# Second attention layer: exponentials transposed by DMA instead of by TensorE, its other DMAs issued by GpSimd

## The chip, the cores and the metric

The kernel runs on one core of one Trainium2 chip. The metric is the device time of one execution in microseconds (us). Engines: TensorE (PE, matmuls; its weight loads are PEld), VectorE (DVE), ScalarE (ACT), GpSimd (POOL) and SyncE (SP), which issues DMAs. All share 16 DMA engines.

## The reference

A model of 1024 tokens with width 1024: one layer with two kinds of attention (differential, and sparse with the 256 best keys), one layer with latent attention (MLA), a norm, and a block of its own with Fourier mixing, windowed attention and 16 experts. The change lies in the second of these, the MLA layer:

```
def block(args):                       # 128 queries; 16 heads
    s = (jnp.einsum('bqhd,bkhd->bhqk', qn, k_nope)
         + jnp.einsum('bqhr,bkr->bhqk', qr, k_rope)).astype(jnp.float32) * scale
    s = jnp.where(chunk_mask(qpos, kpos), s, -jnp.inf)
    p = jax.nn.softmax(s, axis=-1)
    return jnp.einsum('bhqk,bkhd->bqhd', p.astype(v.dtype), v)
...
return x + (o * jax.nn.silu(gate)) @ w_o
```

All in 32 bits. The kernel keeps that accuracy by splitting numbers into a high and a low half: matmuls with fp32r halves take three products, and the product of the exponentials with V has both as pairs of fp16.

## The kernel before

Function `layer1` projects the layer's inputs and stores queries, keys, values and gates in HBM. Then it runs over 16 heads. For each head it loads queries and keys into buffers that alternate between even and odd heads (`load_stack`, L852, and L1212 to L1220), and every fourth head the values (L1223). A head has 8 blocks of 128 queries; block qb sees qb + 1 blocks of keys, so 36 blocks of 128x128 in all. They are taken in five packs (`PACK1`: 7; 6 and 0; 5 and 1; 4 and 2; 3), of 8, 8, 8, 8 and 4 blocks. For each pack:

- TensorE multiplies queries and keys (L293, three products, PSUM banks of 128x512);
- VectorE adds the mask, finds the row maximum and writes the scores to the tile `e` in SBUF (L317; three buffers of `e`);
- ScalarE takes the exponential in place, with the row sum (L1247);
- `p_to_T` transposes `e`: TensorE turns up to four blocks into a PSUM tile `ptp` (L340, 32-bit), ScalarE casts it to fp16 as the high half `pTh` (L341), VectorE subtracts that and writes the rest as the low half `pTl` (L342);
- `pv_mm` multiplies with V: high by high, high by low, low by high (L350 to L352).

Other work is put between the packs: matmuls of the gates (`gate_units`), the preparation of the output weights (`prep_wo`), half of the output product (`half_units`, with loads by `gated_lhs`), bias rows for the next block (`bias_rows`), and modulation rows (`total` in `ada_rows`: load `adx`, one matmul, store to `mod_d`, over one buffer). Every load and store of this stretch is issued by SyncE, in the order of its queue; an instruction that waits holds up those behind it. The order on all engines is made by the framework's scheduler from the order in the text. GpSimd has no work in the heads.

The changed stretch runs from the first loads of keys to the last modulation row, about 1060 to 1490 us of the span.

Of the kernel before, what the change touches and what calls it, by code (L numbers as in the profile page):

```python
# [11 lines left out]
F32 = mybir.dt.float32  # L12
# [82 lines left out]
class K:  # L95


    def __init__(self, ctx, tc):
        self.tc = tc
        self.nc = tc.nc  # L100
        self.ctx = ctx
        self.n = 0
        self.const = ctx.enter_context(tc.tile_pool(name="const", bufs=1))
        self.small = ctx.enter_context(tc.tile_pool(name="small", bufs=3))
        self.dram = ctx.enter_context(tc.tile_pool(name="dscr", bufs=1, space=DRAM))
        nc = self.nc
        self.ident = self.const.tile([P, P], F32, name="ident")
        make_identity(nc, self.ident)
        self.ones = self.const.tile([P, P], F32, name="ones")
        nc.vector.memset(self.ones, 1.0)  # L110
        self.zeros = self.const.tile([P, 1], BF16, name="zeros")
        nc.vector.memset(self.zeros, 0.0)
# [96 lines left out]
    def load_w(self, pool, src, c_list, nk=NK, tag="w", scale=None, hl=None, raw_bufs=1, bufs=None, parts=1):  # L209

        nc = self.nc
        n = sum(w for _, w in c_list)
        if hl is None:
            hl = HL(pool, [P, nk, n], self.nm(tag), tag=tag, bufs=bufs)
        m = nk // parts
        for k0 in range(0, nk, m):
            raw = pool.tile([P, m, n], F32, tag=tag + "_raw", name=self.nm(tag + "raw"), bufs=raw_bufs)
            o = 0
            for c, w in c_list:
                nc.sync.dma_start(raw[:, :, o:o + w], src[k0 * P:(k0 + m) * P, c:c + w].rearrange("(k p) n -> p k n", p=P))  # L220
                o += w
            if scale is None:
                self.split(hl[:, k0:k0 + m], raw)
                continue
            for k in range(m):
                h, l, s = hl.hi[:, k0 + k, :], hl.lo[:, k0 + k, :], scale[:, k0 + k:k0 + k + 1]
                nc.scalar.activation(h, raw[:, k, :], AF.Copy, scale=s)
                nc.vector.scalar_tensor_tensor(l, raw[:, k, :], s, h.bitcast(F32), op0=ALU.mult, op1=ALU.subtract)
        return hl
# [114 lines left out]


def pv_mm(kk, out, hi, lo, v1, v2, nb, off=0):

    mm = kk.nc.tensor.matmul
    for j in range(nb):
        mm(out, hi[:, j, :], v1(off + j), start=j == 0, stop=False)  # L350
        mm(out, hi[:, j, :], v2(off + j), start=False, stop=False)  # L351
        mm(out, lo[:, j, :], v1(off + j), start=False, stop=j == nb - 1)  # L352
# [89 lines left out]
def bias_rows(kk, ps, rel_bias, onehot, heads, ncol, kdim, tag, mul, last=None):  # L442
# [8 lines left out]
    def unit(h, pool):  # L451
        if h == 0:
            rb = at["rb"] = pool.tile([P, heads], F32, name=tag + "rb")
            nc.sync.dma_start(rb[0:32, :], rel_bias)
            nc.vector.tensor_scalar(rb[0:32, :], rb[0:32, :], mul, None, op0=ALU.mult)
            if last is not None:
                nc.vector.memset(rb[32:33, :], last)
            oh = at["oh"] = pool.tile([P, 512], F32, name=tag + "oh")
            nc.sync.dma_start(oh[0:kdim, 0:L + 1], onehot)
        rb, oh = at["rb"], at["oh"]  # L460
# [5 lines left out]
        nc.scalar.copy(sb[:, :L], pb[:, :L])  # L466
        nc.sync.dma_start(scr[h], sb[:, :L])

# [288 lines left out]
def gate_units(kk, ps, pool, W, c0, hT, gate_d, first=None):  # L757
# [15 lines left out]
    def split(c, half):  # L773
        pp, sl = project(first[0] + P * c, half)
        hl = [pool.tile([P, 512], F32, tag="gth", name=kk.nm("gth"), bufs=2).bitcast(F32R) for _ in range(2)]
        kk.split(HL.of(*hl), pp)
        for z, d in zip(hl, first[1]):
            nc.sync.dma_start(d[P * c:P * c + P, sl], z.bitcast(F32))

    def unit(c, half):  # L780
# [3 lines left out]
        nc.vector.scalar_tensor_tensor(th, th, 1.0, pp, op0=ALU.add, op1=ALU.mult)  # L784
        nc.sync.dma_start(gate_d[P * c:P * c + P, sl], th)

# [61 lines left out]
def load_stack(kk, pool, src, row0, tag, lo_first=False, into=None, cols=slice(0, S)):  # L848

    t = pool.tile([P, cols.stop - cols.start], F32R, tag=tag, name=kk.nm(tag), bufs=2) if into is None else into  # L850
    for z in range(2):
        kk.nc.sync.dma_start(t[64 * z:64 * z + 64, :].bitcast(F32), src[z ^ int(lo_first)][row0:row0 + 64, cols])  # L852
    return t
# [17 lines left out]
def load_bias(kk, pool, bias_d, h, ncol, into=None):  # L871
    t = pool.tile([P, ncol], F32, tag="bias", name=kk.nm("bias")) if into is None else into
    L = bias_d.shape[2]
    v = bias_d[h].rearrange("p l -> (p l)")[P - 1:P - 1 + P * (L - 1)].rearrange("(p l) -> p l", l=L - 1)[:, :ncol]
    kk.nc.sync.dma_start(t, v)
    return t
# [28 lines left out]
def prep_wo(kk, pool, w, W, ks, scale=None, colB=None, bufs=2):  # L905
# [6 lines left out]
    def unit(i):  # L912
        for j in range(len(raws), min(i + bufs, len(ks))):
            raws[j] = pool.tile([P, D], F32, tag="woraw", name=kk.nm("woraw"), bufs=bufs)
            nc.sync.dma_start(raws[j], W[ks[j] * P:(ks[j] + 1) * P, :])
        raw, k = raws[i], ks[i]
# [12 lines left out]
def half_units(kk, ps, op, w, lhs, resid, dst):  # L929
# [5 lines left out]
    def unit(t, n):  # L935
# [7 lines left out]
        x = op.tile([P, 512], F32, tag="hx", name=kk.nm("hx"), bufs=2)  # L943
        nc.sync.dma_start(x, resid[rows, cols])
        po = ps.tile([P, 512], F32, tag=MM_BANK[0], name=kk.nm("poh"), bufs=MM_BANK[1])
        for k in range(4):
            kk.mm3(po, lt[t](k), w[k][:, cols], k == 0, k == 3)
        nc.vector.tensor_tensor(x, po, x, op=ALU.add)
        nc.sync.dma_start(dst[rows, cols], x)

# [42 lines left out]
def gated_lhs(kk, ps, op, mix_d, gate_d, k0, bank):  # L993
# [3 lines left out]
    def lhs(t):  # L997
        rows = slice(t * P, (t + 1) * P)
        mx = op.tile([P, 4, P], F32, tag="mx", name=kk.nm("mxt"), bufs=2)
        mv = mix_d[rows, k0 * P:k0 * P + 512].rearrange("p (k c) -> p k c", c=P)  # L1000
        nc.sync.dma_start(mx[:, 0:3], mv[:, 0:3])
        nc.sync.dma_start(mx[:, 3:4], mv[:, 3:4])
        g = op.tile([P, 4, P], F32, tag="gt", name=kk.nm("gtt"), bufs=2)
        nc.sync.dma_start(g, gate_d[k0 * P:k0 * P + 512, rows].rearrange("(k p) s -> p k s", p=P))

# [28 lines left out]
def layer1(kk, ps, a, hT, hold, mix_d, gate_d, wo, mod, wx):  # L1034
# [152 lines left out]
    px.close()  # L1187

    mod2, rows = mod
    ax = ExitStack()  # L1190
# [3 lines left out]
    for i in range(2):  # L1194
        for z in range(2):
            nc.sync.dma_start(kp[64 + 32 * z:96 + 32 * z, i, :].bitcast(F32), kr_d[0])
    k3 = kp[:, 2, :]
    nc.gpsimd.memset(k3[0:64].bitcast(F32), 0.0)
    for z in range(2):
        nc.sync.dma_start(k3[64 + 32 * z:96 + 32 * z, :].bitcast(F32), kr_d[1])  # L1200

# [5 lines left out]
    for h in range(16):  # L1207
# [3 lines left out]
        for z in range(2):  # L1211
            nc.sync.dma_start(k1[64 * z:64 * z + 64, :].bitcast(F32), kn_d[0][r0:r0 + 64, :])  # L1212
        q2 = ap_.tile([P, S], F32R, tag="q2", name=kk.nm("q2"))
        nc.sync.dma_start(q2[0:64, :].bitcast(F32), qn_d[0][r0:r0 + 64, :])
        for i in range(2):
            for z in range(2):
                b = 64 + 32 * i + 16 * z
                nc.sync.dma_start(q2[b:b + 16, :].bitcast(F32), qr_d[z][i][16 * h:16 * h + 16, :])
        k2 = kp[:, h % 2, :]
        at_ = nc.sync.dma_start(k2[0:64, :].bitcast(F32), kn_d[1][r0:r0 + 64, :]).ins  # L1220
        if h % 4 == 0:
            with kk.tc.issue_after(lk[-1]) if h else ExitStack():
                nc.sync.dma_start(vh[:, :, :, r0:r0 + 256], v_d[:, :, :, r0:r0 + 256])  # L1223
        lk.append(at_)
# [4 lines left out]
        for i, pack in enumerate(PACK1):  # L1229
            parts = offsets(pack)  # L1230
            n = parts[-1][2]
            e = ap_.tile([P, S], F32, tag="p", name=kk.nm("e"), bufs=3)
            mx = kk.sm([P, 2], tag="mxc")
# [12 lines left out]
            for z, (qb, c0, c1) in enumerate(parts):  # L1246
                nc.scalar.activation(e[:, c0:c1], e[:, c0:c1], AF.Exp, bias=nm[:, z:z + 1], scale=CS, accum_out=st[:, qb:qb + 1])  # L1247
            hi, lo = p_to_T(kk, ps, ap_, e, n // P)
            for qb, c0, c1 in parts:
# [14 lines left out]
        if h % 2:  # L1264
            nc.sync.dma_start(mix_d[:, (h // 2) * P:(h // 2 + 1) * P].rearrange("(t p) c -> p t c", p=P), o)
        if h == GATES1_HEADS - 1:
# [5 lines left out]
    halves.run()  # L1272
    mod2.run(None, mp)
    ax.close()
    hx.close()

def ada_rows(kk, ps, a, mod_d):
# [4 lines left out]
    c = kk.sm([P, NK], tag="ada_c", bufs=1)  # L1282
    nc.sync.dma_start(c, a["c_2"].rearrange("o (k p) -> p (o k)", p=P))
    th = kk.sm([P, NK], tag="ada_t", bufs=1)
# [7 lines left out]
    def unit(o, ap_, bufs):  # L1292
        acc = ap_.tile([P, H], F32, tag="acc", name=kk.nm("acc"))
        for q in range(0, NK, 2):
            w = ap_.tile([P, 2, H], F32, tag="adw", name=kk.nm("adw"), bufs=bufs)
            nc.sync.dma_start(w, a["w_ada_2"][q * P:(q + 2) * P, o:o + H].rearrange("(k p) n -> p k n", p=P))
            for k in range(2):
# [8 lines left out]
    def total(s, z, dst, gname, ap_):  # L1306
        o = s * D + z * H
        x = ap_.tile([P, H], F32, tag="adx", name=kk.nm("adx"))
        nc.sync.dma_start(x, part_d[:, o:o + H])
        b = ap_.tile([1, H], F32, tag="mb", name=kk.nm("mb"))  # L1310
        nc.sync.dma_start(b, a["b_ada_2"][:, o:o + H])
        pm = ps.tile([P, 512], F32, tag=MM_BANK[0], name=kk.nm("pm"), bufs=MM_BANK[1])
# [4 lines left out]
        if gname:  # L1317
            nc.sync.dma_start(b, a[gname][:, z * H:z * H + H])
            nc.vector.scalar_tensor_tensor(x[0:1, :], x[0:1, :], 1.0, b, op0=ALU.add, op1=ALU.mult)
        nc.sync.dma_start(mod_d[dst:dst + 1, z * H:z * H + H], x[0:1, :])  # L1320

# [847 lines left out]
```

## Time and profile before

| | us |
|---|---|
| median of 3 runs | 2592.82 (2587.34 to 2599.93) |
| the profiled execution | 2589.32 |
| its span, first to last instruction | 2587.5 |
| TensorE busy | 2355.9 (91%) |
| VectorE busy | 1797.5 (69%) |
| ScalarE busy | 1347.5 (52%) |
| GpSimd busy | 438.7 (17%) |
| mean granted TensorE clock | 0.950 |

Busy time is the union of an engine's instructions; issuing DMAs and waiting for semaphores don't count as busy. The clock is given as a share of full speed. A DMA share is the mean busy share of the 16 DMA engines.

### The profile page before, as it was taken

How to read it: one execution, taken by the hardware profiler on the slowest of the kernel's cores; microseconds unless marked ns; L12 is line 12 of the kernel's file. 1: busy time of each engine (PE TensorE's matmuls, PEld its weight loads, DVE VectorE, ACT ScalarE, POOL GpSimd, SP SyncE). 2: the span in 40 equal slices, each digit the busy share in tenths (PEclk: the TensorE clock that was granted, in tenths of full speed). 3: DMA queues.
4: the chain of work that ended last, by engine and by line, in shares of the span. 5: the costliest groups of instructions: out<-in, count | busy, mean ns of one | idle time of the engine just before them, and what ended most of it. 6: DMA issues, size and time to landing. Idle time of an engine off the chain costs nothing.

```text
span 2587.5 us, 40940 instructions
## 1 busy us (share of the span) xinstructions
PE 2355.9 (91%) x14412; PEld 1843.1 (71%) x14412; DVE 1797.5 (69%) x4575; ACT 1347.5 (52%) x2635; POOL 438.7 (17%) x626
## 2 busy tenths in 40 slices
PE   7988888898998878999989979989985999999998
PEld 6866666676777866788767768877864777777776
DVE  4459987877986355366776674677666777777775
ACT  4345675455653333255564375355452666666664
POOL 0000147757740013100000000011000101110110
PEclk9999888899999899999999989989997999999999
DMA  4442476566656227854776461545684999999994
GB/s 131 127 135 79 135 204 184 158 188 191 188 154 208 78 99 258 260 147 123 182 192 170 133 204 55 137 111 163 190 302 184 347 382 351 358 363 374 359 353 137
DMA packets 302637, 523.80 MB, mean 202 GB/s; under 512 B 46022, under 2 KB 191582, under 8 KB 302432
## 3 DMA queue, kind: packets, MB, share of 16 engines
q1 hardware_dynamic: 287456, 467.70, 55.5%
q0 software_dynamic: 14976, 53.49, 6.6%
q8 instruction: 114, 1.87, 0.3%
q14 instruction: 91, 0.75, 0.1%
HBM read 405.18 MB, written 115.65 MB: 201 GB/s over the span
## 4 chain that ended last, share of the span: by engine, by line
PE 61%; DMA 15%; DVE 10%; issue 4%; POOL 4%; ACT 4%; SPq 1%; POOLq 0%; DVEq 0%; ACTq 0%
PE sb L139 6%; PE sb L140 6%; PE sb L141 6%; PE sb L293 5%; PE ptp L340 3%; DMA adw<-w_ada 3%; PE w_gate L1815 2%; PE w_down L1815 2%; PE w_up L1815 2%; DVE tkj L397 2%; PE w_gate L139 2%; PE w_gate L141 2%; PE w_up L139 2%; PE w_up L141 2%; PE w_up L140 2%
## 5 line engine op out<-in xcount | busy, mean ns | idle before, releaser
L341 ACT CAST pTh<-ptp 128x512 f16<-128x512 f32 (+2 forms) x316 | 166.1, 557 | 134.8 <-PE ptp L340 129.0
L342 DVE TENSOR_TENSOR pTl<-ptp,pTh 128x512 f16<-128x512 f32 (+2 forms) x316 | 199.9, 648 | 38.1 <-ACT pTh L341 37.4
L1683 DVE TENSOR_TENSOR ring_l<-mraw,ring_h 128x1024 fp32r<-128x1024 f32 x152 | 183.8, 1223 | 33.6 <-ACT ring_h L1682 31.0
L340 PE MATMUL ptp<-ident,e 128*128 128x128 f32 x1184 | 182.2, 284 | 7.6 <-DVE e L670 2.1
L1682 ACT CAST ring_h<-mraw 128x1024 fp32r<-128x1024 f32 x152 | 156.4, 1048 | 59.0 <-PE w_up L141 20.8
L1683 DVE TENSOR_TENSOR ring_l<-xraw,ring_h 128x1024 fp32r<-128x1024 f32 x136 | 164.7, 1223 | 29.4 <-ACT ring_h L1682 27.0
L1682 ACT CAST ring_h<-xraw 128x1024 fp32r<-128x1024 f32 x136 | 140.7, 1049 | 46.2 <-PE w_up L141 19.9
L340 PEld LDWEIGHTS ptp<-ident,e 128*128 128x128 f32 x1184 | 133.4, 144 | 20.2 <-issue 4.0
L1247 ACT ACTIVATE e<-e,nmx 128x1024 f32<-128x1024 f32 (+7 forms) x128 | 98.4, 770 | 74.5 <-DVE nmx L1245 74.3
L352 PEld LDWEIGHTS <-pTl 128*128 128x128 f16 x1184 | 108.5, 99 | 35.6 <-issue 15.0
L350 PEld LDWEIGHTS <-pTh 128*128 128x128 f16 x1184 | 110.2, 100 | 30.9 <-issue 21.4
L1772 POOL DMA_INDIRECT xg<-h_d,idx x16 | 24.0, 1502 | 598.5 <-DVE gate L1775 550.7
L1298 POOL TENSOR_SCALAR adw<-adw,ada_s 128x256 f32<-128x256 f32 x192 | 109.1, 580 | 93.1 <-DMA adw<-w_ada 92.4
L902 ACT ACTIVATE e<-e,nmx 128x1024 f32<-128x1024 f32 (+7 forms) x128 | 98.5, 772 | 42.7 <-DVE nmx L901 23.4
L351 PEld LDWEIGHTS <-pTh 128*128 128x128 f16 x1184 | 110.0, 99 | 3.9 <-issue 3.2
L293 PE MATMUL sb<-hold_l,q 128*128 128x512 f32 (+3 forms) x384 | 104.0, 359 | 2.0 <-DMA q<-qr 2.0
L317 DVE CUSTOM_DVE_ANT_0 e<-sb,hide 128x512 f32<-128x512 f32 (+3 forms) x128 | 74.5, 583 | 37.6 <-PE sb L293 20.8
L139 PE MATMUL pg<-hold_h,wg_h 128*128 128x512 f32 x192 | 85.7, 446 | 16.3 <-DVE gth L135 14.1
L139 PE MATMUL w_down<-ring_h,hTm_h 128*128 128x512 f32 x192 | 91.3, 476 | 0.0
L139 PE MATMUL w_up<-ring_h,xT_h 128*128 128x512 f32 x192 | 90.3, 470 | 0.0
L139 PE MATMUL w_gate<-ring_h,xT_h 128*128 128x512 f32 x192 | 89.1, 464 | 0.0
L1950 POOL DMA_DIRECT2D xb_d<-x x8 | 4.3, 532 | 496.4 <-DVE rsv L148 448.4
(595 smaller groups left out, 7718.9 us busy)
## 6 DMA issues: line engine op xcount, KB each, us to landing
mraw<-w_up SPq DMA_DIRECT2D x35, 1024.0 KB
mraw<-w_gate SPq DMA_DIRECT2D x34, 1024.0 KB
mraw<-w_down SPq DMA_DIRECT2D x33, 1024.0 KB
xraw<-w_down SPq DMA_DIRECT2D x30, 1024.0 KB
xraw<-w_gate SPq DMA_DIRECT2D x30, 1024.0 KB
xraw<-w_up SPq DMA_DIRECT2D x29, 1024.0 KB
adw<-w_ada SPq DMA_DIRECT2D x96, 256.0 KB
xh_d<-hx SPq DMA_DIRECT2D x48, 256.0 KB
```

Source lines behind the costliest of these rows:

```text
L139: mm(out, a.hi, b.hi, start=start, stop=False)
L140: mm(out, a.hi, b.lo, start=False, stop=False)
L141: mm(out, a.lo, b.hi, start=False, stop=stop)
L293: mm(sc, a, b[:, k0:k0 + n], start=i == 0, stop=i == len(pairs) - 1)
L340: nc.tensor.transpose(pt[:, j, :], p[:, (g + j) * P:(g + j + 1) * P], kk.ident)
L341: nc.scalar.copy(hi[:, g:g + w, :], pt[:, :w, :])
L342: nc.vector.tensor_tensor(lo[:, g:g + w, :], pt[:, :w, :], hi[:, g:g + w, :], op=ALU.subtract)
L350: mm(out, hi[:, j, :], v1(off + j), start=j == 0, stop=False)
L351: mm(out, hi[:, j, :], v2(off + j), start=False, stop=False)
L1682: nc.scalar.copy(w.hi, raw_of(i))
L1683: nc.vector.tensor_tensor(w.lo, raw_of(i), w.hi.bitcast(F32), op=ALU.subtract)
L1815: nc.tensor.matmul(acc[n], xT.full[:, j, :], raw_of(i)[:, j], start=j == 0, stop=False)
```

## The change

`p_to_T` is replaced in the second layer by a function that splits the exponentials in SBUF and lets DMA transposes turn the fp16 halves:

```
+def p_to_T_dma(kk, pool, p, nb):
+    nc = kk.nc
+    n = nb * P
+    hl = pool.tile([P, 2, S], F16, tag="pHL", name=kk.nm("pHL"), bufs=2)
+    hi, lo = [pool.tile([P, NT, P], F16, tag=f"pT_{z}", name=kk.nm("pT" + z), bufs=b) for z, b in (("h", 3), ("l", 2))]
+    nc.scalar.copy(hl[:, 0, :n], p[:, :n])
+    nc.sync.dma_start_transpose(hi[:, 0:nb, :], hl[:, 0, :n])
+    nc.vector.tensor_tensor(hl[:, 1, :n], p[:, :n], hl[:, 0, :n], op=ALU.subtract)
+    nc.sync.dma_start_transpose(lo[:, 0:nb, :], hl[:, 1, :n])
+    return hi, lo
...
-            e = ap_.tile([P, S], F32, tag="p", name=kk.nm("e"), bufs=3)
+            e = ap_.tile([P, S], F32, tag="p", name=kk.nm("e"), bufs=2)
...
-            hi, lo = p_to_T(kk, ps, ap_, e, n // P)
+            hi, lo = p_to_T_dma(kk, ap_, e, n // P)
```

The helpers issue their DMAs on a queue that is a field of the kernel's state. It is SyncE's, except in the stretch, where it is GpSimd's:

```
+        self.q = tc.nc.sync
...
+    kk.q = nc.gpsimd
     mod2, rows = mod
...
     mod2.run(None, mp)
+    kk.q = nc.sync
     ax.close()
```

In the same manner `nc.sync.dma_start` becomes `kk.q.dma_start` in `load_w`, `bias_rows`, `gate_units`, `load_stack`, `load_bias`, `prep_wo`, `half_units`, `gated_lhs`, `ada_rows` and the heads of `layer1`. So in the stretch SyncE issues the 160 transposes and nothing else. The first layer keeps `p_to_T`.

## Rows read from the trace of the kernel before

**Rows 1.** The page's busy us, share of the span and instructions of each engine.

```profile
PE 2355.9 (91%) x14412; PEld 1843.1 (71%) x14412; DVE 1797.5 (69%) x4575; ACT 1347.5 (52%) x2635; POOL 438.7 (17%) x626
```

**Rows 2.** Busy time by stretch; the columns are in the first line.

```profile
core 0: us, PE busy (x) PEld busy (x) DVE busy (x) ACT busy (x) POOL busy (x), PEclk, DMA share, GB/s
1085.00:1490.00 405.00, 383.42 (x3484) 308.37 (x3484) 271.74 (x761) 208.00 (x443) 0.00 (x0) 0.98 0.59 156
...
300.00:350.00 50.00, 34.64 (x118) 23.21 (x116) 45.40 (x169) 33.60 (x62) 12.72 (x25) 0.74 0.81 222
1850.00:1900.00 50.00, 47.90 (x310) 39.55 (x310) 25.99 (x81) 20.87 (x44) 0.21 (x1) 1.00 0.90 314
1900.00:1950.00 50.00, 32.78 (x205) 26.16 (x203) 32.50 (x114) 22.04 (x48) 0.00 (x0) 0.78 0.77 283
1950.00:2000.00 50.00, 30.30 (x134) 21.07 (x135) 34.56 (x81) 14.44 (x21) 2.90 (x2) 0.71 0.33 123
2050.00:2450.00 400.00, 400.00 (x1664) 282.63 (x1663) 311.00 (x425) 260.42 (x355) 43.84 (x22) 1.00 0.98 363
...
0.00:50.00 50.00, 33.46 (x199) 29.30 (x200) 26.57 (x100) 23.09 (x41) 0.71 (x6) 0.97 0.57 165
950.00:1000.00 50.00, 37.33 (x148) 28.22 (x149) 26.71 (x60) 17.71 (x39) 9.87 (x18) 0.90 0.65 227
```

**Rows 3.** Groups by line, 1085 to 1490: busy us, mean ns, idle before.

```profile
L342 DVE TENSOR_TENSOR pTl<-ptp,pTh 128x512 f16<-128x512 f32 x144 | 96.1, 682 | 29.6 <-ACT pTh L341 29.4
L340 PE MATMUL ptp<-ident,e 128*128 128x128 f32 x576 | 88.4, 284 | 2.5 <-ACT e L1247 1.9 <-DVE gtt L1011 0.5
L341 ACT CAST pTh<-ptp 128x512 f16<-128x512 f32 x144 | 79.5, 583 | 64.0 <-PE ptp L340 61.4 <-PE pv L352 2.1
...
L135 DVE TENSOR_TENSOR wg_l<-wgraw,wg_h 128x1024 fp32r<-128x1024 f32 x6 | 7.3, 1221 | 0.3 <-ACT wg_h L134 0.3
...
L134 ACT CAST wg_h<-wgraw 128x1024 fp32r<-128x1024 f32 x5 | 5.2, 1046 | 4.7 <-PE pg L140 4.7
```

**Rows 4.** Waits, 1085 to 1490: us in total, times, longest us.

```profile
ACT pTh L341 <- PE ptp L340: 61.4, 52, 4.1
...
PE pm L1313 <- DMA adx<-ada_d: 14.7, 7, 3.7
```

**Rows 5.** DMA queues and issues, 1085 to 1490: first and last of 24 issue rows.

```profile
DMA packets 50000, 63.34 MB, mean 156 GB/s; under 512 B 4806, under 2 KB 36989, under 8 KB 49957
...
q1 hardware_dynamic: 49957, 62.76, 58.6%
...
hold_l<-kn_hi SPq DMA_DIRECT2D x28, 256.0 KB
...
g2c<-k_norm_g SPq DMA_DIRECT2D x2, 0.2 KB
```

**Rows 6.** DMA issues of GpSimd in the whole span: KB each, median us to landing.

```profile
qn_hi<-pst_h POOLq DMA_DIRECT2D x8, 512.0 KB, 4.2
qn_lo<-pst_l POOLq DMA_DIRECT2D x8, 512.0 KB, 5.1
kn_hi<-pst_h POOLq DMA_DIRECT2D x8, 512.0 KB, 5.3
kn_lo<-pst_l POOLq DMA_DIRECT2D x8, 512.0 KB, 6.0
...
ada_d<-acc POOLq DMA_DIRECT2D x24, 128.0 KB, 3.2
```

**Rows 7.** GpSimd's instructions in order of time: start us, us.

```profile
981.14 0.53 POOL L844 DMA_DIRECT2D qn_hi<-pst_h  x1 [2.87 <-ACT pst_h L134]
981.87 0.53 POOL L845 DMA_DIRECT2D qn_lo<-pst_l  x1 [0.19 <-issue]
```

**Rows 8.** Waits of SyncE's queue, 1050 to 1500.

```profile
SPq L852 <- PE sb L293: 49.2, 12, 10.0
```

**Rows 9.** The chain that ended last, 1085 to 1490, by line.

```profile
by line: PE sb L293 18.0%; PE ptp L340 11.3%; DMA mod_d<-adx 7.8%; DMA adx<-ada_d 6.0%; PE pg L139 5.7%; PE pg L140 5.6%; PE pg L141 5.6%; PE pv L352 3.1%; PE pv L350 2.9%; DMA mix_d<-oc 2.8%; PE pv L351 2.8%; DMA gtt<-gate_d 2.6%; PE pm L1
```

More of the change, by code (lines that the diff above doesn't have):

```diff
@@ L102, in __init__ @@
         self.n = 0
+        self.q = tc.nc.sync
         self.const = ctx.enter_context(tc.tile_pool(name="const", bufs=1))
@@ L219, in load_w @@
             for c, w in c_list:
-                nc.sync.dma_start(raw[:, :, o:o + w], src[k0 * P:(k0 + m) * P, c:c + w].rearrange("(k p) n -> p k n", p=P))
+                self.q.dma_start(raw[:, :, o:o + w], src[k0 * P:(k0 + m) * P, c:c + w].rearrange("(k p) n -> p k n", p=P))
                 o += w
@@ L453, in unit @@
             rb = at["rb"] = pool.tile([P, heads], F32, name=tag + "rb")
-            nc.sync.dma_start(rb[0:32, :], rel_bias)
+            kk.q.dma_start(rb[0:32, :], rel_bias)
             nc.vector.tensor_scalar(rb[0:32, :], rb[0:32, :], mul, None, op0=ALU.mult)
@@ L458, in unit @@
             oh = at["oh"] = pool.tile([P, 512], F32, name=tag + "oh")
-            nc.sync.dma_start(oh[0:kdim, 0:L + 1], onehot)
+            kk.q.dma_start(oh[0:kdim, 0:L + 1], onehot)
         rb, oh = at["rb"], at["oh"]
@@ L466, in unit @@
         nc.scalar.copy(sb[:, :L], pb[:, :L])
-        nc.sync.dma_start(scr[h], sb[:, :L])
+        kk.q.dma_start(scr[h], sb[:, :L])
     for h in range(heads):
@@ L777, in split @@
         for z, d in zip(hl, first[1]):
-            nc.sync.dma_start(d[P * c:P * c + P, sl], z.bitcast(F32))
+            kk.q.dma_start(d[P * c:P * c + P, sl], z.bitcast(F32))
     def unit(c, half):
@@ L784, in unit @@
         nc.vector.scalar_tensor_tensor(th, th, 1.0, pp, op0=ALU.add, op1=ALU.mult)
-        nc.sync.dma_start(gate_d[P * c:P * c + P, sl], th)
+        kk.q.dma_start(gate_d[P * c:P * c + P, sl], th)
     for n, fn in ((4 if first else 0, split), (NK, unit)):
@@ L851, in load_stack @@
     for z in range(2):
-        kk.nc.sync.dma_start(t[64 * z:64 * z + 64, :].bitcast(F32), src[z ^ int(lo_first)][row0:row0 + 64, cols])
+        kk.q.dma_start(t[64 * z:64 * z + 64, :].bitcast(F32), src[z ^ int(lo_first)][row0:row0 + 64, cols])
     return t
@@ L874, in load_bias @@
     v = bias_d[h].rearrange("p l -> (p l)")[P - 1:P - 1 + P * (L - 1)].rearrange("(p l) -> p l", l=L - 1)[:, :ncol]
-    kk.nc.sync.dma_start(t, v)
+    kk.q.dma_start(t, v)
     return t
@@ L914, in unit @@
             raws[j] = pool.tile([P, D], F32, tag="woraw", name=kk.nm("woraw"), bufs=bufs)
-            nc.sync.dma_start(raws[j], W[ks[j] * P:(ks[j] + 1) * P, :])
+            kk.q.dma_start(raws[j], W[ks[j] * P:(ks[j] + 1) * P, :])
         raw, k = raws[i], ks[i]
@@ L943, in unit @@
         x = op.tile([P, 512], F32, tag="hx", name=kk.nm("hx"), bufs=2)
-        nc.sync.dma_start(x, resid[rows, cols])
+        kk.q.dma_start(x, resid[rows, cols])
         po = ps.tile([P, 512], F32, tag=MM_BANK[0], name=kk.nm("poh"), bufs=MM_BANK[1])
@@ L948, in unit @@
         nc.vector.tensor_tensor(x, po, x, op=ALU.add)
-        nc.sync.dma_start(dst[rows, cols], x)
+        kk.q.dma_start(dst[rows, cols], x)
     for t in range(NT):
@@ L1000, in lhs @@
         mv = mix_d[rows, k0 * P:k0 * P + 512].rearrange("p (k c) -> p k c", c=P)
-        nc.sync.dma_start(mx[:, 0:3], mv[:, 0:3])
-        nc.sync.dma_start(mx[:, 3:4], mv[:, 3:4])
+        kk.q.dma_start(mx[:, 0:3], mv[:, 0:3])
+        kk.q.dma_start(mx[:, 3:4], mv[:, 3:4])
         g = op.tile([P, 4, P], F32, tag="gt", name=kk.nm("gtt"), bufs=2)
-        nc.sync.dma_start(g, gate_d[k0 * P:k0 * P + 512, rows].rearrange("(k p) s -> p k s", p=P))
+        kk.q.dma_start(g, gate_d[k0 * P:k0 * P + 512, rows].rearrange("(k p) s -> p k s", p=P))
         def ready():
@@ L1187, in layer1 @@
     px.close()
+    kk.q = nc.gpsimd
     mod2, rows = mod
@@ L1195, in layer1 @@
         for z in range(2):
-            nc.sync.dma_start(kp[64 + 32 * z:96 + 32 * z, i, :].bitcast(F32), kr_d[0])
+            kk.q.dma_start(kp[64 + 32 * z:96 + 32 * z, i, :].bitcast(F32), kr_d[0])
     k3 = kp[:, 2, :]
@@ L1199, in layer1 @@
     for z in range(2):
-        nc.sync.dma_start(k3[64 + 32 * z:96 + 32 * z, :].bitcast(F32), kr_d[1])
+        kk.q.dma_start(k3[64 + 32 * z:96 + 32 * z, :].bitcast(F32), kr_d[1])
     hide = ap_.tile([P, S], BF16, name="hide", bufs=1)
@@ L1211, in layer1 @@
         for z in range(2):
-            nc.sync.dma_start(k1[64 * z:64 * z + 64, :].bitcast(F32), kn_d[0][r0:r0 + 64, :])
+            kk.q.dma_start(k1[64 * z:64 * z + 64, :].bitcast(F32), kn_d[0][r0:r0 + 64, :])
         q2 = ap_.tile([P, S], F32R, tag="q2", name=kk.nm("q2"))
-        nc.sync.dma_start(q2[0:64, :].bitcast(F32), qn_d[0][r0:r0 + 64, :])
+        kk.q.dma_start(q2[0:64, :].bitcast(F32), qn_d[0][r0:r0 + 64, :])
         for i in range(2):
@@ L1217, in layer1 @@
                 b = 64 + 32 * i + 16 * z
-                nc.sync.dma_start(q2[b:b + 16, :].bitcast(F32), qr_d[z][i][16 * h:16 * h + 16, :])
+                kk.q.dma_start(q2[b:b + 16, :].bitcast(F32), qr_d[z][i][16 * h:16 * h + 16, :])
         k2 = kp[:, h % 2, :]
-        at_ = nc.sync.dma_start(k2[0:64, :].bitcast(F32), kn_d[1][r0:r0 + 64, :]).ins
+        at_ = kk.q.dma_start(k2[0:64, :].bitcast(F32), kn_d[1][r0:r0 + 64, :]).ins
         if h % 4 == 0:
             with kk.tc.issue_after(lk[-1]) if h else ExitStack():
-                nc.sync.dma_start(vh[:, :, :, r0:r0 + 256], v_d[:, :, :, r0:r0 + 256])
+                kk.q.dma_start(vh[:, :, :, r0:r0 + 256], v_d[:, :, :, r0:r0 + 256])
         lk.append(at_)
@@ L1264, in layer1 @@
         if h % 2:
-            nc.sync.dma_start(mix_d[:, (h // 2) * P:(h // 2 + 1) * P].rearrange("(t p) c -> p t c", p=P), o)
+            kk.q.dma_start(mix_d[:, (h // 2) * P:(h // 2 + 1) * P].rearrange("(t p) c -> p t c", p=P), o)
         if h == GATES1_HEADS - 1:
@@ L1273, in layer1 @@
     mod2.run(None, mp)
+    kk.q = nc.sync
     ax.close()
@@ L1282, in ada_rows @@
     c = kk.sm([P, NK], tag="ada_c", bufs=1)
-    nc.sync.dma_start(c, a["c_2"].rearrange("o (k p) -> p (o k)", p=P))
+    kk.q.dma_start(c, a["c_2"].rearrange("o (k p) -> p (o k)", p=P))
     th = kk.sm([P, NK], tag="ada_t", bufs=1)
@@ L1295, in unit @@
             w = ap_.tile([P, 2, H], F32, tag="adw", name=kk.nm("adw"), bufs=bufs)
-            nc.sync.dma_start(w, a["w_ada_2"][q * P:(q + 2) * P, o:o + H].rearrange("(k p) n -> p k n", p=P))
+            kk.q.dma_start(w, a["w_ada_2"][q * P:(q + 2) * P, o:o + H].rearrange("(k p) n -> p k n", p=P))
             for k in range(2):
@@ L1308, in total @@
         x = ap_.tile([P, H], F32, tag="adx", name=kk.nm("adx"))
-        nc.sync.dma_start(x, part_d[:, o:o + H])
+        kk.q.dma_start(x, part_d[:, o:o + H])
         b = ap_.tile([1, H], F32, tag="mb", name=kk.nm("mb"))
-        nc.sync.dma_start(b, a["b_ada_2"][:, o:o + H])
+        kk.q.dma_start(b, a["b_ada_2"][:, o:o + H])
         pm = ps.tile([P, 512], F32, tag=MM_BANK[0], name=kk.nm("pm"), bufs=MM_BANK[1])
@@ L1317, in total @@
         if gname:
-            nc.sync.dma_start(b, a[gname][:, z * H:z * H + H])
+            kk.q.dma_start(b, a[gname][:, z * H:z * H + H])
             nc.vector.scalar_tensor_tensor(x[0:1, :], x[0:1, :], 1.0, b, op0=ALU.add, op1=ALU.mult)
-        nc.sync.dma_start(mod_d[dst:dst + 1, z * H:z * H + H], x[0:1, :])
+        kk.q.dma_start(mod_d[dst:dst + 1, z * H:z * H + H], x[0:1, :])
     for s, dst, gname in ((1, 0, "norm_mix_g_2"), (0, 1, None), (2, 2, None), (4, 3, "norm_ffn_g_2"), (3, 4, None), (5, 5, None)):
```

## The prediction

> **What bounds the kernel now.** I read the page's busy shares first: TensorE is busy 91% of the span, VectorE 69%, ScalarE 52% and GpSimd 17% [rows 1]. That is a mean over unlike stages, so I cut out the stage that the change touches, the second layer's attention, from its first loads to its last packs: 1085 to 1490, 405 us for 80 packs (16 heads of 5), 5.06 us each. There TensorE is busy 383 us, VectorE 272, ScalarE 208, GpSimd not at all, and the DMA engines 0.59 of the time [rows 2]. So TensorE sets the pace and has 22 us of idle time. Its groups by line say what it does; the transposes of the exponentials, 576 of them, are 88.4 us of its busy time [rows 3]. The waits agree: ScalarE stands 61.4 us for those transposes, while TensorE's own longest wait is 14.7 us, for the loads of the modulation rows [rows 4]. Last I read the DMA side: 62.8 MB in the stretch, 58.6% of 16 engines, thus 237 us of work if it were packed without gaps, at 265 GB/s [rows 5].
>
> **What the change removes.** 576 transposes of 153 ns of busy time each (88.4/576): TensorE keeps 383 - 88 = 295 us. ScalarE's 144 casts out of PSUM (79.5 us) become 64 casts of 128x1024 and 16 of half the width out of SBUF: 72 full ones at 1.046 us, the row of the same cast for gate weights, 75 us, so -4. VectorE's 144 subtractions (96.1 us) become 72 full ones at 1.221, 88 us, so -8 [rows 3]. Both engines were off the path, so these two I count as nothing; their cover is TensorE now and the DMAs later. If all else were free, the stretch would be bound by TensorE's 295 us and VectorE's 264.
>
> **What it adds: transposes on the DMA engines.** Two per pack, 160 in all: 128 of 256 KB and 32 of 128 KB (the fifth pack of a head has 4 blocks), 1152 blocks of 32 KB, 37.7 MB. That is 60% more bytes than the stretch moves now. The trace shows no DMA transpose, so its price is bounded by rows. From below: in the expert stage plain DMAs move 363 GB/s at a share of 0.98, so 370 when full [rows 2]; 37.7 MB at that rate is 102 us (0.71 us for 256 KB). From above: one at a time, each as long as from issue to landing. 128 KB lands in 3.2 us; the four 512 KB stores just ahead of the stretch, where the DMA share is 0.65, near the 0.59 here, in 4.2, 5.1, 5.3 and 6.0, mean 5.15 [rows 2, 6]; on the straight line between them 256 KB takes 3.85: 128 x 3.85 + 32 x 3.2 = 595 us. Below nothing it can't be: the transposes take no transfer away. The value I take is the slope between those rows, (5.15 - 3.2) us for 384 KB more, 1.3 us for 256 KB (200 GB/s): it is what a further 256 KB costs beside this traffic, and a write that scatters each row over 128 partitions is hardly cheaper than one of whole rows. 144 full ones x 1.3 = 187 us.
>
> The DMA engines then have 237 + 187 = 424 us of work for a stretch of 405. How tightly can it be packed beside TensorE work? The fullest 50 us in which TensorE still ran 47.9 has a share of 0.90 [rows 2]. 424/0.90 = 471 us, +66. The DMA engines become the bound in place of TensorE.
>
> [...]
>
> **What it moves.** The stretch's loads and stores go from SyncE to GpSimd: 329 issues (333 in the list, less 4 of the next stage, which stay) [rows 5]. A GpSimd issue is 0.53 us and the next follows 0.73 after it [rows 7], so 240 us of an engine that does nothing else there. I take nothing for it; its cover is GpSimd's idle time. Issues with many short rows may cost more; at twice the price GpSimd would be full at 480 us, near my stretch. GpSimd's queue inherits SyncE's waits in order: loads of a head two ahead wait for score matmuls to let go of the buffer (49.2 us in 12 waits), and stores and modulation loads queue behind them, as they did on SyncE [rows 8]. The chain through the modulation rows (store, load, matmul) is on the chain that ended last, 7.8% and 6.0% of 405 us [rows 9]; if each of its 24 turns came 1.5 us later and TensorE waited, +36. I take 0, since TensorE gains 176 us of idle time (471 - 295); without that it is up to +36.
>
> SyncE's queue keeps the transposes alone. A transpose of the low part waits there for VectorE's subtraction, and behind it stands only the next pack's high part. One pack's way, cast 1.05, subtraction 1.22, landing 3.85, is 6.1 us; with two buffers of halves it may last two packs (11.8 us at 471), so two buffers do, until a landing takes over 9.5 us. Where the stall on PSUM transposes goes, what is late next is the product with V, which waits for the low half to land.
>
> **TensorE's clock.** At 295 of 471 us it would be 63% busy. [...]
>
> The sum: +66 against the profiled execution (span 2587.5, 2589.3 with what lies around it) is 2655. The median of the runs shown is 2592.8, 3.5 above that execution, so 2659 on its scale.
>
> **The rivals.** A is the forecast. Its own range goes from 1.0 us per 256 KB ((237 + 144)/0.90 = 423, +18) to 2.0 ((237 + 288)/0.90 = 583, +178): 2610 to 2770.
>
> B, one at a time: the queue works off transpose after transpose, each a full landing. Then SyncE's queue alone needs 595 us, +190, 2783; if they also shut out the loads, 595 + 237 = 832, +427, 3020; as with A at 0.90, 661, 2850. For it: each pack's two transposes depend on engines that alternate, so few stand ready at once. Against it: on GpSimd's queue stores issued 0.73 us apart land in 4 to 6, so plain DMAs do overlap. [...]
>
> C, faster: a transpose costs what a plain DMA does in the expert stage. 237 + 102 = 339 us, at 0.90 377, -28, 2565; at 0.98 346, -59, 2534. It decides below 0.89 us for 256 KB, where (237 + 128)/0.90 = 405. TensorE's 295 us, with a little clock lost, fit under it. For it: the halves stay on the chip, while the expert stage's stream reads HBM. Against it: it needs the best rate of the whole trace, and the stretch's own mean is 265 GB/s.
>
> D, no change: the price falls near 0.89 and what TensorE gives, the DMA engines take: 2580 to 2606.
>
> **Chances.** A 0.42, B 0.20, C 0.25, D 0.13. The likeliest is A, so 2659. 0.5% is 13 us, about what a measurement of this kernel can tell from no change: faster 0.25 (C), same 0.13 (D), slower 0.62 (A, B). Cases of both signs hold much, so the range takes in C's middle and most of B: 2560 to 2900, A's own 2610 to 2770.
>
> **What would show it.** Right: the group of the PSUM transposes gone from this stretch, its TensorE busy time near 300 us at clock 1.0 (or longer at a lower clock), the DMA share near 0.9, TensorE's largest wait that of the V product for a transposed half, the stretch 460 to 480 us, the stages behind it unchanged. B would show transposes strung end to end with the share no higher than now. C would show a share of 0.9 in under 385 us. GpSimd issuing without a pause, and scores waiting for q and k loads, would make the moved loads the cause and my zero for them wrong. A PV wait of a few us per pack with a DMA share under 0.7 would say that latency and not the engines' time is the price, and that my packing sum is the wrong model.

## The result and the profile after

The changed kernel takes 2855.9 us in the median (2850.9 to 2867.8, 4 runs) against 2590.1 before: 1.1028 times as long, interval 1.0996 to 1.1061, +266 us. The direction was forecast, the size was not: 2659 with A's own range to 2770. The profiled execution has a span of 2866.0 us.

The stretch is the place. The first store of the next stage (`xb_d`) is issued at 1506.1 us before and at 1774.9 after, 269 later; from there to the end both need the same time to 10 us. Two parts show in the table of stretches: the heads, from the first query product to the last (1084.7 to 1457.2 before, 372 us; 1107.8 to 1637.2 after, 529), and a tail up to the last half product (to 1489 before, to 1759 after). Of the 269 us, 23 are a later start of the heads, 157 their greater length and about 90 the tail. Stretches after; columns as in [rows 2]:

```profile
1107.00:1637.00 530.00, 323.68 (x2563) 245.26 (x2562) 242.34 (x638) 195.53 (x361) 131.63 (x241) 0.74 0.94 160
...
1637.00:1760.00 123.00, 83.71 (x340) 54.70 (x339) 31.69 (x59) 11.04 (x20) 39.74 (x72) 0.81 0.42 124
```

In the heads the DMA engines are nearly full (0.94), TensorE is busy 324 of 530 us, at a granted clock of 0.74 in place of 0.98. In the tail neither is full. The queues of the heads, against [rows 5]:

```profile
DMA packets 162745, 84.54 MB, mean 160 GB/s; under 512 B 151067, under 2 KB 151195, under 8 KB 162707
...
q1 hardware_dynamic: 146902, 36.53, 50.6%
q0 software_dynamic: 15805, 47.52, 43.5%
```

The first of the two is SyncE's queue with the transposes, in packets of 249 bytes in the mean (36.53 MB / 146902); the second is GpSimd's with the loads, in packets of 3.0 KB in the mean. What TensorE waits for in the heads, against [rows 4]:

```profile
PE pv L366 <- DMA pTl<-pHL: 109.5, 27, 16.7
PE pv L364 <- DMA pTh<-pHL: 84.5, 24, 11.6
```

194 us for transposed halves, up to 16.7 in one piece. The groups that took the place of those in [rows 3] cost what was worked out (75.5 us of casts against 75 forecast, 88.7 of subtractions against 88), and they are as idle as forecast, but behind the DMAs:

```profile
L355 DVE TENSOR_TENSOR pHL<-e,pHL 128x1024 f16<-128x1024 f32 (+1 forms) x80 | 88.7, 1114 | 209.3 <-ACT pHL L353 209.1
...
L353 ACT CAST pHL<-e 128x1024 f16<-128x1024 f32 (+1 forms) x80 | 75.5, 956 | 191.4 <-DMA pTl<-pHL 190.8
```

ScalarE's cast waits 190.8 us for the low half's transpose, which has to release the buffer of the pack two before. A transpose takes this long from issue to landing (first the row of its issues, then the landing):

```profile
L354 SPq DMA_TRANSPOSE pTh<-pHL x80: 1189/1240/10700, 1115.7 to 1644.1; - x80
...
DMA to landing us min/median/max: 2.4/4.5/19.8
```

Median 4.5, but up to 19.8 us; for the low half the median is 6.0 and the longest 21.8. One such time, SyncE's queue and GpSimd's in order of time:

```profile
1165.50 3.18 SPq L356 DMA_TRANSPOSE pTl<-pHL  x1
1168.78 9.86 SPq L354 DMA_TRANSPOSE pTh<-pHL  x1
1178.74 4.15 SPq L356 DMA_TRANSPOSE pTl<-pHL  x1
1184.04 1.19 SPq L354 DMA_TRANSPOSE pTh<-pHL  x1
```

```profile
1159.85 0.54 POOL L866 DMA_DIRECT2D hold_l<-qn_hi  x1 [19.86 <-PE sb L294]
1160.38 0.53 POOL L866 DMA_DIRECT2D hold_l<-qn_lo  x1
1160.88 1.04 POOL L1228 DMA_DIRECT2D hold_l<-kn_hi  x2
1161.88 0.54 POOL L1236 DMA_DIRECT2D hold_l<-kn_lo  x1
1162.38 1.23 POOL L1239 DMA_DIRECT2D hold_h<-v_d  x1
```

GpSimd had waited 19.86 us for a buffer and then issued a head's loads in one go. What the queues moved in the 8 us from 1172:

```profile
q0 software_dynamic: 490, 1.61, 96.9%
q1 hardware_dynamic: 416, 0.10, 9.3%
```

Nearly as many packets of each queue, but 1.61 MB of loads against 0.10 MB of transposes: 13 GB/s. In the 12 us before, from 1160, it was 460 packets (1.56 MB) against 1870 (0.47 MB).

The tail is work that before lay between the packs. In the order that the scheduler wrote for TensorE, 15 of the 16 half products stand behind the last head (6 before), and 11 of the 24 modulation products (2 before).

### The profile page after: what moved, and what is told of

Same layout as the page of the kernel before. It is cut to its first block, busy times and chain, and to the rows that moved or that the text cites. A ratio compares the mean times of both kernels' runs of the same rounds, so it can differ in the third digit from the quotient of the medians.

```text
span 2866.0 us, 40131 instructions
## 1 busy us (share of the span) xinstructions
PE 2390.0 (83%) x13836; PEld 1843.1 (64%) x13836; DVE 1798.0 (63%) x4511; ACT 1346.0 (47%) x2571; POOL 636.1 (22%) x982
## 5 line engine op out<-in xcount | busy, mean ns | idle before, releaser
L355 DVE TENSOR_TENSOR pHL<-e,pHL 128x1024 f16<-128x1024 f32 (+1 forms) x80 | 88.7, 1114 | 209.3 <-ACT pHL L353 209.1
L364 PEld LDWEIGHTS <-pTh 128*128 128x128 f16 x1184 | 118.2, 105 | 121.5 <-DMA pTh<-pHL 96.7
L366 PE MATMUL pv<-hold_h,pTl 128*128 128x64 f16 x576 | 74.9, 215 | 111.6 <-DMA pTl<-pHL 111.5
L353 ACT CAST pHL<-e 128x1024 f16<-128x1024 f32 (+1 forms) x80 | 75.5, 956 | 191.4 <-DMA pTl<-pHL 190.8
L364 PE MATMUL pv<-hold_h,pTh 128*128 128x64 f16 x576 | 79.8, 214 | 87.7 <-DMA pTh<-pHL 86.8
L294 PE MATMUL sb<-hold_l,q 128*128 128x512 f32 (+3 forms) x384 | 124.2, 416 | 0.2 <-issue 0.2
L365 PEld LDWEIGHTS <-pTh 128*128 128x128 f16 x1184 | 118.6, 105 | 3.7 <-issue 3.2
L342 ACT CAST pTh<-ptp 128x512 f16<-128x512 f32 (+2 forms) x172 | 87.5, 534 | 69.4 <-PE ptp L341 66.0
L343 DVE TENSOR_TENSOR pTl<-ptp,pTh 128x512 f16<-128x512 f32 (+2 forms) x172 | 104.0, 619 | 10.4 <-ACT pTh L342 10.1
L341 PE MATMUL ptp<-ident,e 128*128 128x128 f32 x608 | 95.6, 290 | 3.6 <-ACT e L916 1.5
L140 PE MATMUL pg<-hold_h,wg_h 128*128 128x512 f32 x192 | 84.1, 438 | 16.3 <-DVE gth L136 14.1
L294 PE MATMUL sb<-hold_l 128*128 128x512 f32 (+1 forms) x192 | 87.8, 459 | 4.6 <-DVE rmx L318 4.2
```

What stands on the lines that cost most here:

```text
L140: mm(out, a.hi, b.hi, start=start, stop=False)
L294: mm(sc, a, b[:, k0:k0 + n], start=i == 0, stop=i == len(pairs) - 1)
L343: nc.vector.tensor_tensor(lo[:, g:g + w, :], pt[:, :w, :], hi[:, g:g + w, :], op=ALU.subtract)
```

## The experiments

Line numbers in expectations are of the kernel named there. "Half product" is one unit of `half_units`. The first run with TensorE's transposes and the first with all DMAs on SyncE split the change in two.

**1. The queue alone.**

```
-            hi, lo = p_to_T_dma(kk, ap_, e, n // P)
+            hi, lo = p_to_T(kk, ps, ap_, e, n // P)      # e with 3 buffers again
```

> The change's second half alone: TensorE transposes as before, the stretch's loads and stores issued by GpSimd. Theories of the +266 us. T1: the DMA engines are full in the heads of the changed kernel (share 0.95 from 1110 to 1640; 36.8 MB of transposes take 269 us of all 16, so 1.87 us for 256 KB and not the 1.3 of the forecast). T2: the engines' time is not the price; each pack waits for the round of its two buffers, and the share is a by-product. T3: a part of the loss, about 110 us (1640 to 1750), is work that the scheduler placed behind the last head (15 of 16 half products, 11 of 24 modulation matmuls), because the stretch's DMAs are in GpSimd's queue. T1 and T2 expect no DMA-bound heads here: 2590 if the queue costs nothing. T3 expects a part of the tail here too, 8 half products and 4 modulation matmuls behind the heads against 6 and 2 before: 2600 to 2640.

Measured 2660.2 us, 1.0272 times before (1.0230 to 1.0314), +70. T1 and T2 alone would have it at 2590, and T3's band ends 20 lower. The heads last 396 us, with the DMA share at 0.54 and a last half product at 1543. So issuing the same DMAs from GpSimd, in the order that the scheduler then writes, costs 70 us. TensorE's waits, 1096 to 1543, against [rows 4]:

```profile
PE pm L1330 <- DMA adx<-ada_d: 33.8, 11, 5.4
```

The chain through the modulation rows holds TensorE up for 33.8 us in place of 14.7.

**2. The transposes alone.**

```
-    kk.q = nc.gpsimd
```

> The change's first half alone: all 160 DMA transposes, but every other load and store of the stretch back on SyncE's queue, among them. No half product is placed behind the heads. T1: DMA work 237 + 269 = 506 us, at 0.95 a stretch of 533 against 405 before, +128, and up to 20 us at its start: 2720 to 2750. T3 agrees that the tail goes. T2, and the rival that transposes must not stand behind loads in a queue: in SyncE's queue a transpose stands behind loads that wait for score matmuls (49 us in 12 waits before), each round gets longer, so slower than the changed kernel, over 2860.

Measured 2694.0, 1.0400 (1.0361 to 1.0439), +104: 26 below T1's band, and at least 166 below what T2 and the rival wanted. Its heads:

```profile
1088.00:1562.00 474.00, 365.51 (x2792) 269.33 (x2791) 267.21 (x678) 200.43 (x364) 0.00 (x0) 0.84 0.96 207
```

```profile
q1 hardware_dynamic: 193555, 97.76, 96.0%
```

```profile
PE pv L364 <- DMA pTh<-pHL: 34.6, 25, 4.5
PE pv L366 <- DMA pTl<-pHL: 26.8, 28, 2.6
```

The DMA engines are as full as in the changed kernel, but move more in less time (97.76 MB in 474 us, since all half products are in the heads, against 84.05 in 530), and no wait for a half is over 4.5 us. Here transposes stand behind the loads in one queue, and that is better than beside them in two (2694 us against 2856). The two halves of the change add up to 70 + 104 = 174; together they cost 266, 92 more.

**3. Half of the transposes, on the changed kernel.**

```
-    nc.sync.dma_start_transpose(lo[:, 0:nb, :], hl[:, 1, :n])
-    return hi, lo
+    return hi, hi
```

> As the changed kernel, but the low half is not transposed and the high half stands in for it in the third product (left out: the low half of the exponentials). 80 transposes in place of 160. T1: DMA work of the heads 231 + 135 = 366 us, at 0.95 385 us in place of 530, so -145 and about 2710, the tail as in the changed kernel (16 half products behind the heads). T2: a round loses the subtraction (1.1 us) and the later of two landings (6.0 against 4.5), 2.6 of about 8 us, so a third of the heads' extra length: -50, about 2805.

Measured 2798.4 (1.0832, 1.0767 to 1.0897), -57: T1 is 88 off and T2 within 7. The heads last 467 us at a DMA share of 0.78, so the engines are not full and yet TensorE waits 146.4 us for the high half, up to 17.5 in one piece:

```profile
PE pv L363 <- DMA pTh<-pHL: 146.4, 35, 17.5
```

Full engines are not the whole cause in the changed kernel. T2 has no place for 17.5 us either, as a round of its buffers is about 8.

**4. Few loads, on the changed kernel.**

```
+        if h < 2:
             q1, k1, q2, k2 loads of the head
```

> As the changed kernel, with all 160 transposes and the same buffers, but query and key loads for the first two heads alone; later heads reuse them (left out: the other 14 heads' queries and keys, 25 MB). 4 half products behind the heads. T1: the loads of the heads go down from 231 us of DMA work by about 121; with 269 of transposes and the half products' transfers (60) back among the heads 440, at 0.95 463, and no tail: about 2660. The time of all engines for a transpose stays near 1.87 us for 256 KB, which is then its own price and not that of the loads beside it. T2: the rounds of the two buffers stay, only the tail goes: 2740 to 2760.

Measured 2646.5 (1.0210, 1.0167 to 1.0252): near T1's 2660, not T2's 2740. With the buffers as they were, the heads last 402 us and landings shrink to 4.0 and 4.1 in the median. Whatever the cause is, the loads beside the transposes are in it. But this also cleared most of the tail (4 half products behind the heads), so it does not tell a full engine from a starved queue.

**5 and 6. Which loads, in which queue.** Do the late transposes go with the head loads in the other queue? First these loads back in the transposes' queue, then the other way round:

```
+        kk.q = nc.sync        # run 6: nc.gpsimd
         loads of q1, k1, q2, k2 and vh
+        kk.q = nc.gpsimd      # run 6: nc.sync
```

> As the changed kernel, but the loads of queries, keys and values of each head go back to SyncE's queue, with the transposes; the rest of the stretch (gates, half products, modulation rows) stays on GpSimd's. [...] In this kernel 8 half products are behind the heads (15 in the changed kernel). T1: DMA work as in the run with all on SyncE, so about 2700 and 20 to 30 for the tail, 2720 to 2730. [...] T3 alone (the tail gone, heads as in the changed kernel, 530): 2780.

> The other way round: the head loads on GpSimd's queue, all else of the stretch on SyncE's with the transposes; 4 half products behind the heads, no modulation rows. T1: as the run with all on SyncE, 2690 to 2710, since the bytes and the transposes are the same. [...]

Measured 2727.4 (1.0544, 1.0515 to 1.0573) and 2767.0 (1.0697, 1.0674 to 1.0720). The first lies in T1's band. The second lies 57 above T1's, which ends at 2710. Its heads last 527 us, as long as the changed kernel's, with nearly the same tail as run 2. TensorE's waits in the heads, run 5, then run 6:

```profile
PE pv L364 <- DMA pTh<-pHL: 41.2, 20, 5.4
PE pv L366 <- DMA pTl<-pHL: 37.5, 28, 3.2
```

```profile
PE pv L366 <- DMA pTl<-pHL: 77.1, 21, 15.5
PE pv L364 <- DMA pTh<-pHL: 63.7, 17, 9.7
```

The long waits come and go with the head loads in the other queue. But T1 is not refuted by that: its band took the engines' work to be the same as in run 2, and it was not. The queues of run 6's heads:

```profile
DMA packets 183969, 93.25 MB, mean 177 GB/s; under 512 B 150211, under 2 KB 171642, under 8 KB 183930
...
q1 hardware_dynamic: 174602, 63.90, 65.5%
q0 software_dynamic: 9328, 28.84, 27.8%
```

Their packets took 93.3% of 527 us, 492 us for 92.74 MB, where run 2's took 455 us for 97.76 MB. So by this measure the heads of run 6 are nearly as full as those of run 2, with packets that take longer. (It is a sum of the packets' times, and those of two queues can overlap: in the 8 us above the shares add up to 106%.) Whether the transposes are late because the other queue's packets go first, or because all packets take longer beside another queue's, this pair doesn't tell.

**7. The packets of that queue.** Run 6 with each load of q and k cut in two by columns, to see whether the size of that queue's packets makes the heads long.

```
+        for c in (slice(0, 512), slice(512, S)):
             loads of [..., c]
```

> As the run with the head loads alone on GpSimd's queue (2767, heads 527 us, longest wait for a transposed half 15.5 us), but each of these loads is cut into two of half the columns: the same bytes and nearly the same order (5 half products behind the heads, 4 there), rows of 2 KB in place of 4 KB. [...] The rival, that the order or the issuing engine and not the packets makes the heads long: no shorter, 2765 to 2790, as 96 more GpSimd issues of 0.55 us each only add work.

Measured 2756.5 (1.0632, 1.0601 to 1.0662), 10 us less than run 6 and below the rival's band (from 2765). The heads lasted 524 us against 527. But the edit did not make the packets smaller. The same 527 us as in run 6:

```profile
DMA packets 184047, 92.59 MB, mean 176 GB/s; under 512 B 150526, under 2 KB 171869, under 8 KB 184007
...
q0 software_dynamic: 10672, 28.85, 30.0%
```

Of 2 KB and more there are 12138 packets here (184007 - 171869) and 12288 in run 6 (183930 - 171642). In the trace's records GpSimd's queue has 7040 packets of 4096 bytes in both runs, all of its bytes but 0.01 MB; what grew are packets of 4 bytes, from 2288 to 3632, as there are more DMAs. So what smaller packets do was not tested by this run. The longest wait of TensorE's weight loads for the low half did fall, from 16.3 to 7.4 us, and their sum from 87.9 to 69.0, with the same packets in more and smaller DMAs; the heads are hardly shorter, at a share of 0.99. That speaks for the engines' time as the bound of these heads more than for the long waits; it is an argument and not a test.

**8 and 9. What the queue costs without transposes.** TensorE's transposes, with the head loads alone on GpSimd, then with all else alone on it.

```
-            hi, lo = p_to_T_dma(kk, ap_, e, n // P)
+            hi, lo = p_to_T(kk, ps, ap_, e, n // P)      # on runs 6 and 5
```

> TensorE transposes as before the change, only the head loads on GpSimd's queue. It splits the +70 of the queue's move without DMA transposes. Placed behind the heads: 5 half products, no modulation rows (before: 6 and 2). If the +70 comes from the small work (modulation rows, half products) on GpSimd's queue, T3: 2585 to 2605 here. If it comes from the head loads there: 2640 to 2660.

> The other part: TensorE transposes, head loads on SyncE's queue, the small work (gates, half products, modulation rows, bias rows) on GpSimd's. Behind the heads: 8 half products and 4 modulation rows. If the small work there is the cause of the +70: 2635 to 2660. If the head loads are: 2590 to 2605.

Measured 2626.7 (1.0141, 1.0114 to 1.0167) and 2632.6 (1.0160, 1.0132 to 1.0188): +34 and +40, together 74 beside the 70 of run 1. The first is between its bands, the second just under the upper one: neither single cause holds. With the head loads there, the first query product is at 1094.8 (1084.7 before) and the heads last 398 us; with the small work there, the heads last 377, but start at 1097.0 and the last half product is at 1529 (1489 before). So about half of the 70 comes with the head loads, as a later start and a slower pace of the heads, and half with the small work, as a later start and work that ends late. The head loads' packets in run 8's heads (398 us), to be read beside run 6's:

```profile
q0 software_dynamic: 9328, 28.84, 30.5%
```

The same 9328 packets took 121 us of all engines here, without DMA transposes, and 147 us in run 6, beside them.

**10 and 11. Room on the DMA engines, with one queue.** Run 2 with the high half alone, and with few loads.

```
-    kk.q = nc.gpsimd          # on runs 3 and 4
```

> As the run with all DMAs on SyncE's queue (2694, DMA share 0.96 over 474 us of heads, 455 us of work), but the high half alone is transposed and stands in for the low one (left out: the low half of the exponentials). Nothing is behind the heads and no second queue has bursts. T1: the engines' work falls by half of the transposes' 230 us, to 340, at 0.96 354 us, so -120 and 2570 to 2590, unless TensorE's own 300 us at a lower clock take longer. The rival (T2, rounds of the buffers, and waits in SyncE's queue behind loads): the gain is that of one landing and a subtraction, -50 or less, 2640 to 2690.

> As the run with all DMAs on SyncE's queue, with all 160 transposes, but query and key loads for the first two heads alone (left out: the other heads' queries and keys, 25 MB). T1: work falls by some 105 us (25 MB at the 240 GB/s or so of these loads) to 350, at 0.96 365 us, so -110 and about 2580; the price of a transpose of 256 KB shows with little beside it, 1.6 us or less. T2: the transposes' rounds are unchanged, 2660 to 2690.

Measured 2628.5 (1.0146, 1.0120 to 1.0173) and 2618.7 (1.0109, 1.0071 to 1.0148), -66 and -75 against run 2. Both fall between the theories. The stretches of the heads (first to last query product 1088 to 1508, and 1103 to 1494):

```profile
1086.00:1500.00 414.00, 339.20 (x2752) 259.87 (x2751) 256.91 (x669) 199.29 (x366) 0.00 (x0) 0.88 0.84 193
```

```profile
1086.00:1490.00 404.00, 340.44 (x2748) 252.97 (x2748) 260.41 (x669) 199.29 (x365) 0.00 (x0) 0.90 0.84 178
```

Taking work off the DMA engines helped here, which fits their fullness as the bound of run 2. But at 0.84 they are no longer full, and the heads (420 and 391 us) are still longer than the 372 before although TensorE has lost its 576 transposes. It waits 41.1 us for the high half in the first of these runs and has a clock of 0.88. What else keeps the heads from T1's 354 and 365 us is not settled.

The first of them prices a transpose. Its queue:

```profile
q1 hardware_dynamic: 118779, 79.22, 84.0%
```

84.0% of 414 is 348 us for 79.22 MB, run 2's 96.0% of 474 is 455 us for 97.76: the 18.5 MB of low halves cost 107 us of all engines, 1.51 us for 256 KB, 173 GB/s. For all 160 (37.7 MB) it would be 218 us.

**12 and 13. A version that might beat both.** One pack in five through DMA transposes, all DMAs on SyncE's queue, the pack of 8 blocks 5 and 1, or the last of 4 blocks:

```
+            hi, lo = p_to_T_dma(kk, ap_, e, n // P) if i in VIA_DMA else p_to_T(kk, ps, ap_, e, n // P)
```

> A version that may beat both: of each head's five packs one, 5 and 1 with 8 blocks, goes through DMA transposes, the other four through TensorE; all loads and stores on SyncE's queue as before the change, one buffer for the split exponentials. TensorE is relieved of 128 transposes (20 us), the DMA engines get 32 transposes of 256 KB at 1.6 to 1.9 us, 51 to 60 us, to their 237, a share of 0.73 of 405. T1: there is room, so up to 20 us faster, 2575 to 2590. The rival: a transpose stands in SyncE's queue behind loads that wait, or holds those behind it up, and TensorE's gain is lost: 2590 to 2620.

> The same with the smallest pack, block 3 with 4 blocks, the last of each head: TensorE is relieved of 64 transposes (10 us), the DMA engines get 32 transposes of 128 KB, 26 to 30 us. T1: up to 10 us faster, 2580 to 2592. The rival (waits in SyncE's queue, or the end of a head waiting for a landing): 2590 to 2610.

Measured 2598.8 (1.0039, 1.0024 to 1.0054) and 2600.9 (1.0056, 1.0036 to 1.0077): no gain, 10 and 12 us slower, both within the rivals' bands. In the first, the heads last 366 us in its profile against 372 before, at a share of 0.74, so the few us won there don't reach the end. No version tried beats the kernel before.

## Why the prediction was wrong

**What was right.** The direction; TensorE as the bound before; its transposes gone; the price of the casts and subtractions; the DMA engines as the new bound; TensorE's largest waits those of the V product. For the transposes alone the sum comes near, with two errors that partly cancel. Run 2's first `xb_d` is at 1605.2, 99 us after the kernel before, so the stretch that ended at 1490 ends at 1589 there:

```profile
1085.00:1589.00 504.00, 376.74 (x2895) 277.47 (x2895) 274.94 (x697) 208.93 (x380) 0.00 (x0) 0.83 0.94 203
```

```profile
q1 hardware_dynamic: 201943, 101.86, 93.6%
```

That is 504 us where 471 were forecast, with 472 us of packets (93.6%): 235 more than the 237 before, where 187 were taken, at a share of 0.94, where 0.90 was taken. The 2694 of run 2 lies in A's range, 35 over its 2659.

**The mis-sized price** belongs to this smaller part: 1.3 us for 256 KB by the slope between rows of stores, against 1.51 (run 2 less run 10) to 1.63 (run 2 less the kernel before, 235 us for 144). Rival C, with the 370 GB/s of the expert stage, does not hold here: 160 to 173 GB/s, while the stretch's plain DMAs moved 265 before. Rival B, one at a time, is not what happens: 160 transposes of median landing 4.5 and 6.0 us would make some 840 us, and the heads last 529. That 2850 was also B's number is chance. By the 1.51, a block of 32 KB costs 0.19 us of all engines.

**The step that failed** is the one on what the change moves: "I take nothing for it; its cover is GpSimd's idle time". GpSimd had that time (132 us busy of 530 in the heads, all of it DMA issues, which count as busy on this engine), and most DMAs there cost 0.48 to 0.56 us as counted; the sign that the prediction named for a mistake here, GpSimd issuing without a pause, did not come. What was left out is where the queue stands and not what it costs to feed. The move is worth 70 us by itself (run 1) and 162 beside transposes (2856 - 2694). The rows show three ways:

- The modulation chain got slower, as the text had bounded by +36 and then covered with TensorE's idle time: 33.8 us of waits in place of 14.7 in run 1, where that cover did not exist.
- The scheduler wrote another order, with half products behind the heads. The tail of the changed kernel lasts 122 us against 32, with TensorE waiting for the short chains of this work (22.9 us in 8 waits for `adx` loads). The prediction took the order as given; "the stages behind it unchanged" was true, but the stretch itself grew a stage.
- Two queues at work at once held each other up. In the 8 us shown, bursts of loads in packets of some 3 KB left 13 GB/s to transposes in packets of some 250 bytes. Beside one queue of mixed work (run 2) the longest wait for a half is 4.5 us, beside head loads in the other queue 15.5 and 16.7 (run 6 and the changed kernel). The prediction did not ask which queue gets the engines, and its limit for two buffers, "until a landing takes over 9.5 us", was passed by landings of up to 19.8 and 21.8. The packets also took longer: 499 us in the changed kernel's heads (94.1% of 530) for 84.05 MB, 455 us in run 2's for 97.76, and the same head loads 147 us beside transposes (run 6), 121 without (run 8). So the 237 us that the prediction took over from before for the loads did not hold beside transposes in another queue either.

How the 92 us of the interaction divide between the tail, the bursts and the longer packets is open: run 6 less run 2 is 73 us with little tail, but 34 of that the head loads cost on GpSimd without any transpose (run 8). No run changed the packets' sizes, so the bursts of large packets as the cause of the late transposes are argued from run 3, runs 5 and 6 and the 8 us shown, and not shown by a run of their own.

**The clock** was 0.74 at 61% busy, as in one of the stretches of [rows 2]. The prediction allowed for that ("or longer at a lower clock") and its sum takes nothing for it; that it stays hidden behind the DMAs is not shown. TensorE's busy time in the whole span is 2390.0 us against 2355.9 before, although 88.4 us of transposes went, so its other work took some 122 us longer; no run tells how much of that lengthened the kernel.

## What to carry to other kernels

Before work is moved to the DMA engines, add up their time in that stretch: at a share of 0.6 there was no room for 60% more bytes, and the gain of 88 us on TensorE could not come through. Before transfers are given a queue of their own, look at the packets on both sides: here a queue of small packets (249 bytes in the mean) that TensorE waits for fell behind beside bursts of large ones (3.0 KB) in another queue, with waits of up to 16.7 us, and it was better off behind them in the same queue (up to 4.5 us, and 2694 against 2856). And when a scheduler writes the order, a change of queues changes the order of everything that hangs on them, so compare the orders, not only the costs.

## What was not expected of the hardware

SBUF-to-SBUF transposes moved 160 to 173 GB/s of all 16 engines' time, in packets of 249 bytes in the mean, and issuing one took 1.24 us of SyncE's queue in the median for the high half, up to 10.7 (plain loads there before mostly took 0.2 to 0.6). In 8 us of one burst GpSimd's queue got 490 packets of 3.3 KB in the mean and SyncE's 416 of 0.24 KB. The same loads on GpSimd's queue took 121 us of all engines without transposes and 147 beside them. Cutting these loads into rows of half the length left the queue's packets at 4 KB.
